# A two-layer hybrid encoder on one core: the matrix-inverse bursts ordered behind the query-key products, a free slot between two of them, an early square-root table, and wider last multiplications

## The chip, the core and the metric

The kernel runs on one core of a Trainium2 chip, in float32. The metric is device microseconds of one execution. The kernel before took 2420.61 us, the median of three runs (2418.82, 2420.61 and 2422.45).

## The reference

Two layers work on 1040 rows (16 meta tokens and 1024 tokens) of width 1024. Each layer normalises its rows, projects them once, and splits the projection between a gated delta rule of 4 heads in both directions and a gated short convolution; both go through one output projection into the residual. A SwiGLU block of 22 tiles of 128 follows. Of the delta rule, this matters here:

```
q, k, v, g, beta = (to_chunks(t) ...)            # chunks of 64 in the reference
decay_mat = exp(where(incl, G_i - G_j, -inf))
M = where(strict, (k*beta) k^T * decay_mat, 0);  A = M + I
u = A^-1 (v*beta);  w = A^-1 (k*beta*exp(G))     # the triangular inverse
attn = (q k^T) * decay_mat                       # the query-key products
step: v_new = u - w S;  o = (q*exp(G)) S + attn v_new;  S = S*gl + k_dec^T v_new
o = (o_fwd + o_bwd);  o = o * rsqrt(mean(o*o) + eps)
...
h = rmsnorm(h, final_norm_w);  return h[:, N_META:]
```

## The kernel before, in words

Everything is stored transposed, with channels on the 128 partitions and rows along the free dimension. A dense product keeps float32 accuracy by splitting each operand in a rounded part and a remainder: `dense` issues three matmuls per k tile (lines 174, 175 and 176) into a PSUM bank `pacc` (or `pf`), over column chunks of 348, 346 and 346 (layer 0) or 512, 512 and narrower ones (layer 1). Weights arrive by SyncE's queue (line 137), are split by ScalarE (line 138) and VectorE (line 139), and go into a ring of three.

The small work of the delta rule is done under these dense products. The chunks here are of 128 rows, nine in all, the first with the 16 meta rows. Three lists of jobs, `jobs`, `jobs2` and `jobs3`, are emptied by `slot()` inside `dense`, one entry of each list per slot; `None` is a free slot. A projection of three chunks has three slots, after each 24 matmuls. So the lists set where small work stands between dense work, and a priority (`mmp`, moved on by `low`) keeps it there when the scheduler orders each engine's instructions. The order on an engine is in the end that of the scheduler, by priorities and by its own estimate of when operands are ready; it then is fixed in the program.

`jobs2` holds, from the first z projection on, the query-key products: `chunk_a(c)` issues four 128x128 products per chunk (line 597), loads the two directions' decay matrices on GpSimd's queue (line 600), multiplies on VectorE (line 601) and stores the result to DRAM (line 602).

`jobs3` holds the inverse of the 128x128 triangular matrices, by blocks of 32, of both directions and all chunks at once (`invert`). Its matmuls are short and come in bursts: the first form (`first(0)` and `first(1)`, line 677) has 64 products of 32x32 in each half; the second and third form (lines 692 and 693) have four parts of 48; the fourth and the fifth (lines 718 and 738) have 64 of 64x64 each. float32 operands that are not rounded go through TensorE in two passes, so that 64 such products are 128 matmuls and 128 weight loads in the trace. Each burst is given to `low(f, hold=True)`, which orders its first matmul behind the last dense matmul issued so far (`after(one, last_mm[0])`); nothing orders it against query-key products.

Then comes the scan over the chunks (`scan_step`, all its matmuls on line 968, the meta chunk's on 1047), the two directions interleaved, nine steps. From step 4 on the second direction to reach a chunk finishes it (`finalize`): the first one's output is stored to DRAM (`od`, line 1028) and loaded back (line 1102), VectorE takes off the state's part (line 1103) and adds the PSUM bank (line 1104), ScalarE squares and sums (line 1108), then takes the square root (line 1110), for which it first loads another activation table; VectorE takes the reciprocal and scales (lines 1111 and 1112), TensorE transposes (line 1114). The bank that line 1104 reads is the one that the next step's second state product of that direction writes. ScalarE copies with a scale on lines 996, 1004 and 1005 serve each step. `St` is the state, `qs` the state's part of the output, `vv` the new values, `b3f`/`a3f` the row that is finished.

At the very end of layer 1 the rows are multiplied by the final norm's factor, in three column parts. For the last part (256 columns) eight multiplications of 128x256 follow a reciprocal (line 1900), six on VectorE and two on GpSimd (line 1863), and eight stores go out in turn on SyncE's and ScalarE's queues (line 1864). Line 1974 stands for what closes the program: each engine drains and all meet.

Of the kernel before, what the change touches and what calls it, by code (L numbers as in the profile page):

```python
# [7 lines left out]
F32 = mybir.dt.float32  # L8
# [7 lines left out]
KT = 8  # L16
NMETA = 16
L = 1040
H = 4
# [23 lines left out]
def trunk(ctx: ExitStack, tc: tile.TileContext, xT, w_in, w_ba, w_out, w_gu, w_dn,  # L43
# [41 lines left out]
    def after(ins, prev):  # L85

        if prev is not None:
            tc.add_manual_dep(ins.ins, prev.ins.name, dep, reason="order")
        return ins

    def at_prio(p):
        tc.cur_priority = p
# [239 lines left out]
    for l in range(DEPTH):  # L332
# [258 lines left out]
        def chunk_a(c):  # L591

            if c == 0:
                return None if last else chunk_a0()
            n, s0 = span(c)
            qk = bank("b").rearrange("p (h i) -> p h i", h=4)
            low(lambda: [mm(qk[0:n, h, 0:n], KTt[:, h, s0:s0 + n], QT[:, h, s0:s0 + n], start=True, stop=True) for h in range(H)])
            for d in (0, 1):
                dt_ = t2k("dt")
                qdma(dt_[0:n, :, 0:n], dtd[c, d].rearrange("p (h i) -> p h i", h=4)[0:n, :, 0:n])  # L600
                tt(out=dt_, in0=qk[0:n, :, 0:n], in1=dt_[0:n, :, 0:n], op=ALU.mult)
                dma(aqd[c, d], dt_.rearrange("p a b -> p (a b)"))
# [2 lines left out]
        B = [slice(32 * b, 32 * b + 32) for b in range(4)]  # L605

        inv = {}

        def sub_start():

# [24 lines left out]
        def invert():  # L635
# [5 lines left out]
            def turn_back(d):  # L641
                rows, cols = (Xi[:, d], Xi[:, d].rearrange("p i c -> p c i"))[::1 - 2 * d]
                after(nc.vector.transpose(out=XB[d].rearrange("p q c -> p c q"), in_=cols), evacs[-1])
                nc.vector.transpose(out=ZB[:, d].rearrange("p q i -> p i q"), in_=rows)
                for b in range(4):
                    act(out=Pv[d][B[b], :, B[b]], in_=ZB[B[b], d], func=AF.Copy)
# [6 lines left out]
            def fill():  # L653
                for d, f, s in (pairs[0], pairs[2]):
                    fo, so = 32 * (f % 2), 32 * (s % 2)
                    nc.vector.tensor_copy(XF[B[f], :, fo:fo + 32], XB[d][B[f]])
                    nc.vector.tensor_copy(XF[B[s], :, so:so + 32], XB[d][B[s]])
                    nc.vector.memset(XF[B[f], :, so:so + 32], 0.0)
# [10 lines left out]
            def first(part):  # L669
                if part == 0:  # L670
                    banks_["1"] = [view(bank("f"), 32) for _ in halves]
                pss = banks_["1"]

                def turn(q):
                    out = []
                    for i in range(2):
                        out += [mm(pss[i][B[s ^ 2 * i], q, :], Pv[d][B[f], 16 * i + q, B[s]], XB[d][B[f], 16 * i + q, :], **kw) for (d, f, s) in pairs]
                    return out

                low(lambda: [turn(q) for q in range(8 * part, 8 * part + 8)][0][0], True)  # L680
                if part == 1:
                    act(out=QS[:, halves[0], :], in_=pss[0], func=AF.Copy, scale=-1.0)
                    act(out=QS[H64[0], halves[1], :], in_=pss[1][H64[1]], func=AF.Copy, scale=-1.0)
                    act(out=QS[H64[1], halves[1], :], in_=pss[1][H64[0]], func=AF.Copy, scale=-1.0)
# [44 lines left out]
            def fifth():  # L729
# [12 lines left out]
                for j in range(4):  # L742
# [5 lines left out]
                        else:  # L748
                            nc.vector.tensor_copy(to, ps)

            return ([lambda: turn_back(0), lambda: (turn_back(1), fill()), None] + [lambda i=i: first(i) for i in range(2)] + [None] + [lambda qs=qs, i=i: second_third(qs, i) for qs in halves for i in range(2)]
                    + [None, fourth, None, fifth])

        l2s = {}
# [102 lines left out]
        def low(f, hold=False):  # L857

            here = tc.cur_priority
            at_prio(mmp[0])  # L860
            one = f()
            if hold:
                after(one, last_mm[0])
            mmp[0] = tc.cur_priority
            at_prio(here)

        def v_store(i, v, c0):

# [71 lines left out]
        bk = [[bank("f"), bank("f")], [bank("b"), bank("b")]]  # L940
        fin = row(Y[1] + "f")
        nfin = [0]
        done = set()
        read = {}

# [5 lines left out]
        def scan_step(d, c, first, final, tied=False, behind=None):  # L951
            n, s0 = 128, 16 + 128 * (c - 1)
            base = (1 - d) * 2048
            V, K, A, sz = (rec[:, base + 512 * i:base + 512 * i + 512].rearrange("p (h e) -> p h e", h=4) for i in range(4))
            dma(V[0:n].rearrange("p h e -> p (h e)"), vkd[c, 0:n, 0, :])
            if not final:
                dma(K[0:n].rearrange("p h e -> p (h e)"), vkd[c, 0:n, 1, :])
            dma(A.rearrange("p h e -> p (h e)"), aqd[c, d])
            Zs = [Pv[d][:, (c - 1) * 4 + h, :] for h in range(4)]
            As = [A[:, h, :] for h in range(4)]  # L960
            b0, b1 = (v4(t) for t in bk[d])
            opened = [None]

            def group(ph):
                opened[0] = ph

            def gm(*args, **kw):
                one = mm(*args, **kw)  # L968
                if opened[0] is not None and tied:
                    after(one, ready[1 - d].get(opened[0]) if tied == 1 else ends[1 - d])  # L970
                if opened[0] == "A":
                    after(one, behind)
                opened[0] = None
                ends[d] = one
                return one

            vv = vvs[d]
            vn, vs = v4(vv[:, 0:512]), v4(vv[:, 512:1024])
            if first:
                r = V  # L980
            else:
                ks = b0
                group("A")
                for h in range(H):
                    gm(ks[0:n, h, :], KTt[:, h, s0:s0 + n], St[d][:, h, :], start=True, stop=True)
                r = vn
                for h in range(H):
                    ready[d]["B"] = stt(out=r[0:n, h, :], in0=ks[0:n, h, :], scalar=negE[0:n, d, c, h:h + 1], in1=V[0:n, h, :], op0=ALU.mult, op1=ALU.add)
            qs = None
            if not first:  # L990

                qs = qso[d]
                for h in range(H):
                    gm(b1[0:n, h, :], QT[:, h, s0:s0 + n], St[d][:, h, :], start=True, stop=True)
                for h in range(H):
                    act(out=qs[0:n, h, :], in_=b1[0:n, h, :], func=AF.Copy, scale=negE[0:n, d, c, h:h + 1])
            yield
            vr = b1
            group("B")
            for h in range(H):  # L1000
                gm(vr[0:n, h, :], Zs[h], r[0:n, h, :], start=True, stop=True)
            for h in range(H):
                if not final:
                    ready[d]["C"] = act(out=vs[0:n, h, :], in_=vr[0:n, h, :], func=AF.Copy, scale=bkd[0:n, d, c, h:h + 1])
            ready[d]["C"] = read[d, c] = act(out=vn[0:n], in_=vr[0:n], func=AF.Copy)
            yield
            group("C")
            if not final:
                su = b0
                for h in range(H):  # L1010
                    gm(su[:, h, :], K[0:n, h, :], vs[0:n, h, :], start=True, stop=True)
            po = b1
            for h in range(H):
                gm(po[0:n, h, :], As[h], vn[0:n, h, :], start=True, stop=True, skip_group_check=True)
            if not final:
                for h in range(H):
                    if first:
                        ready[d]["A"] = nc.vector.tensor_copy(St[d][:, h, :], su[:, h, :])
                    else:
                        ready[d]["A"] = stt(out=St[d][:, h, :], in0=St[d][:, h, :], scalar=gl[:, d, c, h:h + 1], in1=su[:, h, :], op0=ALU.mult, op1=ALU.add)  # L1020
            pof = po.rearrange("p h e -> p (h e)")
            if c not in done:
                done.add(c)
                if first:
                    act(out=vs.rearrange("p h e -> p (h e)"), in_=pof, func=AF.Copy)
                else:
                    tt(out=vs, in0=po, in1=qs, op=ALU.subtract)
                dma(od[c], vs.rearrange("p h e -> p (h e)"))
            else:
                finalize(c, n, s0, pof, qs, sz)  # L1030
# [820 lines left out]
        else:  # L1851
# [46 lines left out]
                    pend = [lambda q=q, n0=n0, n1=n1, mul=tt if n0 == 16 and q > 5 else ptt: scaled(q, n0, n1, mul, ss[:, n0:n1], dma) for q in range(KT)]  # L1898
            act(out=sv, in_=ps[:, 0:n1 - n0], func=AF.Sqrt, scale=1.0 / D, bias=cols["eps"])
            nc.vector.reciprocal(out=sv, in_=sv)  # L1900
            for q in range(KT):
                scaled(q, n0, n1, ptt if q in (3, 6) else tt, sv, (dma, adma)[q % 2])
        if not last:
            finish_bc(ss, 0, L, rsd[1])
        hsrc = hd
# [73 lines left out]
```

## Time and profile before

| | |
|---|---|
| runs | 2418.82, 2420.61, 2422.45 us |
| profiled execution | 2422.96 us, span 2421.1 us |
| TensorE busy (matmul, weight load) | 2401.0 us (99%), 2225.8 us (92%) |
| VectorE, ScalarE, GpSimd busy | 1836.5, 1043.6, 89.7 us |
| mean granted TensorE clock | 0.997 |
| moved by DMA | 336.57 MB, 139 GB/s |
| first bursts of the inverse, line 677 | 228.5 to 1453.6 us, 512 matmuls in both layers |

A row of the timeline gives start, length, engine, line, operation, the tiles written and read, the shape and how many instructions are merged; in square brackets stands how long the engine was idle before it and what ended that. Matmuls overlap, so the distance of two starts is what a matmul costs, not its length. Times are counted from the span's start; layer 0's inverse runs at 228 to 262 us, its scan to about 490 us, and layer 1's inverse begins at 1440 us.

### The profile page before, as it was taken

To read this page: it belongs to the slowest core of one execution; us is meant where nothing else is said; L and a number is where in the kernel's file an instruction comes from. 1 tells how busy PE (TensorE), PEld (TensorE's weight loads), DVE (VectorE), ACT (ScalarE), POOL (GpSimd) and SP (SyncE) were. 2 spreads that over 40 slices of the span, in tenths; PEclk is the share of its full clock that TensorE was granted. 3 is DMA by queue.
4 is the path that set the end of the run, shared out by engine and by line. 5 is a ranking of instruction groups with operands and counts; after the bars stand their busy time and mean duration, and the time that the engine had idled before them with its cause. 6 is when DMAs were issued, how large, how long until landed. Compare 5 with 4: busy or idle time off the path is not lost.

```text
span 2421.1 us, 44848 instructions
## 1 busy us (share of the span) xinstructions
PE 2401.0 (99%) x17507; PEld 2225.8 (92%) x17507; DVE 1836.5 (76%) x3322; ACT 1043.6 (43%) x1959; POOL 89.7 (4%) x195
## 2 busy tenths in 40 slices
PE   9999999999999999999999999999999999999998
PEld 8999999999999999999999988998988888888887
DVE  7798545768888877877658985457898887778775
ACT  6654334436233333444446432335553343334544
POOL 0141000000000000000001200000000000000002
PEclk9999999999999999999999999999999999999999
DMA  4455444633222224674224445446433232347641
GB/s 136 147 164 177 164 137 139 200 112 130 93 100 86 101 74 136 223 254 142 88 87 152 156 151 174 140 136 213 138 114 111 81 111 79 121 154 246 198 126 70
DMA packets 198023, 336.57 MB, mean 139 GB/s; under 512 B 22972, under 2 KB 88692, under 8 KB 197812
## 3 DMA queue, kind: packets, MB, share of 16 engines
q1 hardware_dynamic: 174324, 294.06, 36.6%
q10 hardware_dynamic: 18464, 25.85, 3.1%
q0 software_dynamic: 5024, 13.82, 1.9%
q8 instruction: 137, 2.24, 0.4%
q14 instruction: 74, 0.61, 0.1%
HBM read 251.52 MB, written 82.12 MB: 138 GB/s over the span
## 4 chain that ended last, share of the span: by engine, by line
PE 93%; DVE 3%; DMA 2%; issue 1%; ACT 1%; SPq 0%; DVEq 0%; ACTq 0%
PE pacc L174 10%; PE pacc L176 10%; PE pacc L175 10%; PE pacc L1269 4%; PE pacc L1273 4%; PE pacc L1272 4%; PE pb L1273 3%; PE pb L1269 3%; PE pb L1272 3%; PE pf L1269 3%; PE pf L1273 3%; PE pf L1272 3%; PE pf L968 3%; PE pb L968 3%; PE pacc L1837 2%; PE pacc L1836 2%
## 5 line engine op out<-in xcount | busy, mean ns | idle before, releaser
L174 PE MATMUL pacc<-a,whi 128*128 128x346 f32 (+1 forms) x800 | 261.1, 327 | 0.6 <-ACT a L210 0.4
L176 PE MATMUL pacc<-a,wlo 128*128 128x346 f32 (+1 forms) x800 | 259.5, 325 | 0.1
L174 PE MATMUL pacc<-b,whi 128*128 128x342 f32 (+3 forms) x672 | 232.3, 346 | 0.0
L176 PE MATMUL pacc<-b,wlo 128*128 128x342 f32 (+3 forms) x672 | 230.6, 344 | 0.0
L175 PE MATMUL pacc<-a,whi 128*128 128x346 f32 (+1 forms) x681 | 221.8, 326 | 0.5 <-DVE a L211 0.5
L138 ACT ACTIVATE whi<-raw 128x512 fp32r<-128x512 f32 x166 | 104.7, 631 | 249.1 <-PE pacc L175 179.7
L175 PE MATMUL pacc<-b,whi 128*128 128x342 f32 (+3 forms) x580 | 199.7, 344 | 0.0
L139 DVE TENSOR_TENSOR wlo<-raw,whi 128x512 fp32r<-128x512 f32 x166 | 114.1, 687 | 63.1 <-ACT whi L138 61.6
L174 PEld LDWEIGHTS pacc<-a,whi 128*128 128x128 f32 x800 | 151.0, 189 | 3.6 <-issue 1.5
L176 PEld LDWEIGHTS pacc<-a,wlo 128*128 128x128 f32 x800 | 151.0, 189 | 1.3 <-issue 0.6
L174 PEld LDWEIGHTS pacc<-b,whi 128*128 128x128 f32 x672 | 126.4, 188 | 10.3 <-issue 1.7
L176 PEld LDWEIGHTS pacc<-b,wlo 128*128 128x128 f32 x672 | 126.5, 188 | 9.8 <-issue 1.5
L175 PEld LDWEIGHTS pacc<-a,whi 128*128 128x128 f32 x681 | 128.7, 189 | 4.7 <-issue 1.9
L175 PEld LDWEIGHTS pacc<-b,whi 128*128 128x128 f32 x580 | 109.2, 188 | 7.2 <-issue 1.1
L1251 ACT ACTIVATE whi<-rw 128x512 fp32r<-128x512 f32 (+1 forms) x84 | 51.7, 620 | 105.4 <-PE pacc L1272 28.2
L1251 ACT ACTIVATE b<-rw 128x512 fp32r<-128x512 f32 (+1 forms) x63 | 38.8, 620 | 89.9 <-PE pb L1272 35.3
L1251 ACT ACTIVATE a<-rw 128x512 fp32r<-128x512 f32 (+1 forms) x63 | 38.5, 619 | 71.0 <-PE pacc L1272 29.3
L351 DVE TENSOR_TENSOR a<-pacc,rstd 128x342 f32<-128x342 f32 (+3 forms) x59 | 32.4, 553 | 38.3 <-PE pacc L176 36.9
L1252 DVE TENSOR_TENSOR wlo<-rw,whi 128x512 fp32r<-128x512 f32 (+1 forms) x84 | 56.2, 672 | 6.6 <-ACT whi L1251 6.2
L1837 PE MATMUL pacc<-P,wlo 128*128 128x260 f32 (+1 forms) x177 | 59.4, 336 | 0.0
L1836 PE MATMUL pacc<-P,whi 128*128 128x260 f32 (+1 forms) x177 | 59.3, 335 | 0.0
L1834 PE MATMUL pacc<-P,whi 128*128 128x260 f32 (+1 forms) x177 | 59.2, 335 | 0.0
(1178 smaller groups left out, 7858.2 us busy)
## 6 DMA issues: line engine op xcount, KB each, us to landing
raw<-in_w_in SPq DMA_DIRECT2D x110, 256.0 KB
raw<-in_w_gu SPq DMA_DIRECT2D x106, 256.0 KB
rw<-in_w_gu SPq DMA_DIRECT2D x90, 256.0 KB
rw<-in_w_dn SPq DMA_DIRECT2D x90, 192.0 KB
raw<-in_w_out SPq DMA_DIRECT2D x48, 256.0 KB
b<-ad SPq DMA_DIRECT2D x45, 260.0 KB
a<-ad SPq DMA_DIRECT2D x45, 256.0 KB
ad<-a SPq DMA_DIRECT2D x20, 520.0 KB
```

The lines of the kernel that those rows point to most:

```text
L138: whi_done[0] = hasten(wpr, lambda: act(out=hi, in_=raw[:, 0:kk, :], func=AF.Copy))
L139: whi_done[1] = hasten(wpr, lambda: tt(out=lo, in0=raw[:, 0:kk, :], in1=hi.bitcast(F32), op=ALU.subtract))
L174: mm(ps[:, :n], wh, xh[:, n0:n1], start=(seen[0] == 1), stop=False)
L175: mm(ps[:, :n], wh, xl[:, n0:n1], start=False, stop=False)
L176: last_mm[0] = mm(ps[:, :n], wl, xh[:, n0:n1], start=False, stop=(seen[0] == K))
L968: one = mm(*args, **kw)
L1251: hasten(wpr, lambda: act(out=hi, in_=src, func=AF.Copy))
L1269: one = mm(ps[:, :CW], w[0][:, k, :], th[:, cs], start=first and k == 0, stop=False, skip_group_check=True)
L1272: mm(ps[:, :CW], w[0][:, k, :], tl[:, cs], start=False, stop=False, skip_group_check=True)
L1273: one = mm(ps[:, :CW], w[1][:, k, :], th[:, cs], start=False, stop=stop and k == nk - 1, skip_group_check=True)
L1836: mm(ps[:, :CW], wh[:, k, :], tl[:, cs], start=False, stop=False, skip_group_check=True)
L1837: mm(ps[:, :CW], wl[:, k, :], th[:, cs], start=False, stop=en, skip_group_check=True)
```

## The change

Four edits. `chunk_a` keeps the last of its four products in `qk_last`, and `low(f, hold=True)` orders the burst's first matmul behind that product too. In `invert`'s list a free slot stands between `first(0)` and `first(1)`, so all that follows in `jobs3` comes one slot later. In the scan, at step 4 of direction 0, ScalarE takes the square root of a constant into a new tile `root`, ordered behind that step's last copy of line 996. At the end, the last column part is multiplied by five VectorE instructions, three of two rows of tiles at once (128x2x256) and two of one, with five stores; GpSimd has no part in it.

```
-            low(lambda: [mm(qk[0:n, h, 0:n], ...) for h in range(H)])
+            qk_last[0] = low(lambda: [mm(qk[0:n, h, 0:n], ...) for h in range(H)])[-1]
...
-  ... + [lambda i=i: first(i) for i in range(2)] + [None] + ...
+  ... + [lambda: first(0), None, lambda: first(1), None] + ...
...
             if hold:
                 after(one, last_mm[0])
+                after(one, qk_last[0])
...
+            halfway = c == 4 and d == 0
...
                 for h in range(H):
-                    act(out=qs[0:n, h, :], in_=b1[0:n, h, :], func=AF.Copy, scale=negE[0:n, d, c, h:h + 1])
+                    copied = act(out=qs[0:n, h, :], in_=b1[0:n, h, :], func=AF.Copy, scale=negE[0:n, d, c, h:h + 1])
+                if halfway:
+                    after(act(out=root, in_=epsc, func=AF.Sqrt), copied)
...
-            for q in range(KT):
-                scaled(q, n0, n1, ptt if q in (3, 6) else tt, sv, (dma, adma)[q % 2])
+            for i, (q, w) in enumerate(((0, 2), (2, 2), (4, 2), (6, 1), (7, 1))):
+                h = hb[q // 4][:, q % 4:q % 4 + w, n0:n1]
+                tt(out=h, in0=h, in1=sv.unsqueeze(1).to_broadcast([128, w, n1 - n0]), op=ALU.mult)
+                (dma, adma)[i % 2](out[q:q + w, :, n0 - 16:n1 - 16].rearrange("q p e -> p q e"), h)
```

What it moves is seen in the order of the engines' instructions. TensorE, layer 0, in the first half of the inverse's first form; `pf` are the burst's banks, `pb` those of the query-key products of two chunks. Before:

```order
L677 MATMUL pf_2492<-e_2170,P_853 32x32 x2
L677 MATMUL pf_2492<-e_2171,P_854 32x32 x2
L677 MATMUL pf_2493<-e_2170,P_853 32x32
L597 MATMUL pb_2389<-b_36_211,b_37_212 128x128 x4
L677 MATMUL pf_2493<-e_2170,P_853 32x32
L677 MATMUL pf_2493<-e_2171,P_854 32x32 x2
L677 MATMUL pf_2492<-e_2170,P_853 32x32 x2
L677 MATMUL pf_2492<-e_2171,P_854 32x32 x2
L677 MATMUL pf_2493<-e_2170,P_853 32x32 x2
L677 MATMUL pf_2493<-e_2171,P_854 32x32
L597 MATMUL pb_2479<-b_36_211,b_37_212 128x128 x4
```

And now, where the burst's line is 678 by the added lines:

```order
L176 MATMUL pacc_2558<-a_3_74,wlo_2422 128x346
L597 MATMUL pb_2389<-b_36_211,b_37_212 128x128 x4
L597 MATMUL pb_2479<-b_36_211,b_37_212 128x128 x4
L678 MATMUL pf_2492<-e_2170,P_853 32x32 x2
L678 MATMUL pf_2492<-e_2171,P_854 32x32 x2
L678 MATMUL pf_2493<-e_2170,P_853 32x32 x2
```

Both groups of query-key products now stand ahead of the burst, behind ten more dense matmuls, and its 64 products follow one another. Between the two halves stood 10 dense matmuls; now 24 do, and one more group of four. In layer 1 two groups and two groups of transposes (line 882) stood within the first half and one group within the second; none does now, and 31 dense matmuls and one group stand between the halves.

VectorE, layer 0, around the first chunk that is finished (step 4 of the scan); `b3f` is the row that is finished, `pf_4175` the bank that its next state product writes, `vv_4173` serves the other direction. Before:

```order
L364 SCALAR_TENSOR_TENSOR b_403_3794<-b_384_3612,par,b_403_3794 128x1039
L1103 TENSOR_TENSOR b3f_4178<-b3f_4178,qs_4170 128x512
L365 SCALAR_TENSOR_TENSOR b_403_3794<-b_384_3612,par,b_403_3794 128x1039
L988 SCALAR_TENSOR_TENSOR vv_4173<-pb_4176,negE_585,b_180_1491 128x128 x4
L1103 TENSOR_TENSOR b3f_4178<-b3f_4178,qs_4171 128x512
L1104 TENSOR_TENSOR b3f_4178<-pf_4175,b3f_4178 128x512
```

And now, seven lines further down in the file:

```order
L365 SCALAR_TENSOR_TENSOR b_403_3794<-b_384_3612,par,b_403_3794 128x1039
L1110 TENSOR_TENSOR b3f_4178<-b3f_4178,qs_4170 128x512
L1111 TENSOR_TENSOR b3f_4178<-pf_4175,b3f_4178 128x512
L993 SCALAR_TENSOR_TENSOR vv_4173<-pb_4176,negE_585,b_180_1491 128x128 x4
L1110 TENSOR_TENSOR b3f_4178<-b3f_4178,qs_4171 128x512
L993 SCALAR_TENSOR_TENSOR vv_4172<-pf_4174,negE_585,b_180_1491 128x128 x4
```

The addition that frees the bank follows its subtraction at once. On TensorE the product that writes this bank stood 41 dense matmuls behind the three products ahead of it, and now stands 17 behind them; those three stand 27 dense matmuls behind the step before, where there were 22.

ScalarE at the same place, before and now, with the square root's table:

```order
L996 ACTIVATE qs_4171<-pb_4177,negE_585 128x128 x4
L1108 ACTIVATE pa_4557,st_4558<-b3f_4178 128x128 x4
L1110 ACT_TABLE_LOAD
L1110 ACTIVATE st_4558<-st_4558 128x4
L996 ACTIVATE qs_4170<-pf_4175,negE_585 128x128 x4
```

```order
L1001 ACTIVATE qs_4170<-pf_4175,negE_585 128x128 x4
L1003 ACT_TABLE_LOAD
L1003 ACTIVATE root_4179<-epsc 128x1
L1011 ACTIVATE vv_4173<-pb_4177,bkd_587 128x128 x4
```

The table is loaded one step earlier, behind the copies of line 996 (now 1001) and ahead of those of line 1004 (now 1011); there are as many table loads as before.

More of the change, by code (lines that the diff above doesn't have):

```diff
@@ L596, in chunk_a @@
             qk = bank("b").rearrange("p (h i) -> p h i", h=4)
-            low(lambda: [mm(qk[0:n, h, 0:n], KTt[:, h, s0:s0 + n], QT[:, h, s0:s0 + n], start=True, stop=True) for h in range(H)])
+            qk_last[0] = low(lambda: [mm(qk[0:n, h, 0:n], KTt[:, h, s0:s0 + n], QT[:, h, s0:s0 + n], start=True, stop=True) for h in range(H)])[-1]
             for d in (0, 1):
@@ L607, in trunk @@
         inv = {}
+        qk_last = [None]
         def sub_start():
@@ L749, in fifth @@
                             nc.vector.tensor_copy(to, ps)
-            return ([lambda: turn_back(0), lambda: (turn_back(1), fill()), None] + [lambda i=i: first(i) for i in range(2)] + [None] + [lambda qs=qs, i=i: second_third(qs, i) for qs in halves for i in range(2)]
+            return ([lambda: turn_back(0), lambda: (turn_back(1), fill()), None] + [lambda: first(0), None, lambda: first(1), None] + [lambda qs=qs, i=i: second_third(qs, i) for qs in halves for i in range(2)]
                     + [None, fourth, None, fifth])
@@ L863, in low @@
                 after(one, last_mm[0])
+                after(one, qk_last[0])
             mmp[0] = tc.cur_priority
             at_prio(here)
+            return one
         def v_store(i, v, c0):
@@ L942, in trunk @@
         nfin = [0]
+        root = sb.tile([128, 1], F32, tag="root", name=nm("root"))
         done = set()
```

## The prediction

> **What bounds the kernel now.** I read the page first: busy time, code queue and chain.
>
> ```profile
> span 2421.1 us, 44848 instructions
> PE 2401.0 (99%) x17507; PEld 2225.8 (92%) x17507; DVE 1836.5 (76%) x3322; ACT 1043.6 (43%) x1959; POOL 89.7 (4%) x195
> q8 instruction: 137, 2.24, 0.4%
> PE 93%; DVE 3%; DMA 2%; issue 1%; ACT 1%; SPq 0%; DVEq 0%; ACTq 0%
> ```
>
> TensorE is busy for 99% and 93% of the chain is its own. The change leaves every matmul in, so only three things can move the time: moments in which TensorE stands still, stretches in which it runs slowly, and the end, where it is done. The view of waits, TensorE's alone, names the moments:
>
> ```profile
> PE pf L677 <- issue: 1.6, 1, 1.6
> PE pa L1114 <- ACT qs L996: 1.4, 1, 1.4
> PE pf L968 <- DVE b3f L1104: 0.6, 1, 0.6
> ```
>
> The longest lies in the inverse's burst, with no engine behind it ("issue"); the next two lie at one step of the scan. All three places are touched.
>
> **The bursts of layer 0.** TensorE's timeline there:
>
> ```profile
> 228.45 0.33 PE L677 MATMUL pf<-e,P 32*32 32x32 f32 x26
> 228.72 1.16 PE L597 MATMUL pb<-b,b 128*128 128x128 f32 x8
> 229.81 0.31 PE L677 MATMUL pf<-e,P 32*32 32x32 f32 x20
> 230.18 1.13 PE L597 MATMUL pb<-b,b 128*128 128x128 f32 x8
> 231.23 0.90 PE L677 MATMUL pf<-e,P 32*32 32x32 f32 x82
> 232.07 0.43 PE L176 MATMUL pacc<-a,wlo 128*128 128x346 f32 x1
> 233.86 0.92 PE L677 MATMUL pf<-e,P 32*32 32x32 f32 x85
> 236.38 0.57 PE L677 MATMUL pf<-e,P 32*32 32x32 f32 x43 [1.60 <-issue]
> 236.89 0.42 PE L174 MATMUL pacc<-a,whi 128*128 128x348 f32 x1
> 242.34 1.05 PE L597 MATMUL pb<-b,b 128*128 128x128 f32 x8
> ```
>
> The same stretch in the view of windows (length, TensorE, weight load, VectorE, ScalarE, GpSimd, granted clock, DMA share, GB/s), and what the code queue moved from 233.8 to 234.8 us:
>
> ```profile
> 234.80:236.40 1.60, 0.02 (x4) 0.02 (x4) 0.00 (x0) 0.00 (x0) 0.60 (x2) 1.00 1.00 297
> 236.40:237.80 1.40, 1.40 (x49) 1.36 (x50) 0.60 (x1) 0.00 (x0) 0.00 (x0) 1.00 0.89 309
> 237.80:241.30 3.50, 3.50 (x14) 3.50 (x14) 3.50 (x6) 2.83 (x4) 0.54 (x1) 0.51 0.81 284
> ```
>
> ```profile
> q8 instruction: 1, 0.02, 5.5%
> ```
>
> I read the pause as a wait for code. TensorE's 17507 matmuls and as many weight loads are 35014 instructions, and queue 8 moved 137 packets, so one packet is 256 instructions. Half a first form (26 + 20 + 82 matmuls with their loads) is one whole packet, used up in little over a microsecond. One packet was moving just before the pause ended, with the DMA engines at a share of 1.00. Counting 128 matmuls back from the pause: 85 of the second half, 10 dense, 33 of the first half's last 82, so the packet that ran out was begun at about 231.7 us, the next arrived at 236.4, and the way from asking to having took at most about 4.6 us here. A packet must last that long.
>
> Then from 237.8 us for 3.5 us the granted clock is 0.51: 14 matmuls where there is room for 22. About half of the 3.5 us is lost, 1.7 us.
>
> [...]
>
> **The change there.** Ten more dense matmuls and two groups of four products (16 matmuls, two passes each) now come ahead of the first burst, so that the packet's start, formerly 33 matmuls from the end of the first half, lies 59 from it. Up to the next packet's start come: 59 matmuls of the first half (0.6 us at 0.84 us for 82, from 231.23 to 232.07), 24 dense (3.8 us: 0.16 each, from the 10 between 232.07 and 233.86 with their change-over), one group (0.9 us: 0.8 to the next dense start and 0.1 for a slower successor), and 37 of the second half (0.4): 5.7 us against at most 4.6. The pause goes: **-1.6 us**, and with it the half-clock stretch: **-1.7 us**. The margin is 1.1 us; DMA work hides nothing here, it is what could lengthen the way of the code. The free slot's own cost is nil on TensorE: the dense products that fill it are the same ones, earlier; what is late next by it, the fourth and fifth form, starts the scan within a few dense matmuls of where it stood.
>
> Interrupted bursts also cost. The second half without its pause takes 236.89 - 233.86 - 1.60 = 1.43 us; a group between dense ones 0.9. So the first half should take 1.43 + 1.8 = 3.23, and took 3.62 (228.45 to 232.07): 0.4 lost. Layer 1:
>
> ```profile
> 1440.66 0.24 PE L677 MATMUL pf<-e,P 32*32 32x32 f32 x2
> 1440.84 0.66 PE L882 MATMUL pa<-ident,a3f 128*128 128x128 f32 x4
> 1445.54 0.50 PE L174 MATMUL pacc<-b,whi 128*128 128x512 f32 x1
> 1451.26 0.26 PE L677 MATMUL pf<-e,P 32*32 32x32 f32 x6
> 1453.71 0.50 PE L174 MATMUL pacc<-b,whi 128*128 128x512 f32 x1
> ```
>
> The first half takes 4.88 us with two groups of products and two of transposes inside (about 0.5 each): 4.23 expected, 0.65 lost. The second takes 2.45 against 2.33: 0.1. Together **-1.2 us**, between 0 (if the change-overs are paid wherever the groups stand) and 1.5.
>
> **The scan's step 4.** VectorE, TensorE and ScalarE in layer 0:
>
> ```profile
> 385.01 1.06 PE L968 MATMUL pf<-S,b 128*128 128x128 f32 x8
> 388.94 0.69 DVE L1103 TENSOR_TENSOR b3f<-b3f,qs 128x512 f32<-128x512 f32 x1 [4.21 <-DMA b3f<-od]
> 392.39 0.68 DVE L1104 TENSOR_TENSOR b3f<-pf,b3f 128x512 f32<-128x512 f32 x1
> 393.13 1.16 PE L968 MATMUL pf<-S,b 128*128 128x128 f32 x8 [0.56 <-DVE b3f L1104]
> 394.83 1.28 ACT L1110 ACT_TABLE_LOAD   x1
> 396.57 0.69 DVE L1112 TENSOR_TENSOR b3f<-b3f,st 128x512 f32<-128x512 f32 x1
> 397.41 0.63 PE L1114 MATMUL pa<-ident,b3f 128*128 128x128 f32 x4 [1.39 <-ACT qs L996]
> ```
>
> TensorE stands 0.56 us for line 1104, then 1.39 us for a transposition that waits through the table load (the releaser named, line 996, came after the root on ScalarE; the data came from line 1112). In the new order the table load lies between copies that wait for TensorE anyway, and its 1.28 us are off this path: the transposition stands 17 dense matmuls and one group of products behind the bank product and should wait 0.2 at most. But the product on the bank now comes 17 dense matmuls after 385.9 us plus 0.8 us for the five that moved ahead: TensorE is there at about 389.4. The row lands at 388.94, perhaps 0.3 later since line 364 now stands ahead of the state update, and lines 1103 and 1104 now run back to back (1.3 us): the bank is free at 390.5. So TensorE waits 1.1 us here. Net: 1.95 before, 1.3 after, **-0.6 us**; the ends are -1.9 (all hidden) and +2 (row later by 2.6 us). Layer 1 shows no wait at this step, and its bank product moves five dense matmuls back: nothing.
>
> **The end.** From the timeline, and from the views of lines 1863 and 1974 (count: shortest/median/longest ns, first and last start):
>
> ```profile
> 2404.94 4.72 POOL L1863 TENSOR_TENSOR b<-b,rstd 128x256 f32<-128x256 f32 x6
> ...
> 2410.47 1.75 DVE L1900 RECIPROCAL rstd<-rstd 128x256 f32<-128x256 f32 x1 [1.75 <-ACT rstd L1899]
> 2412.26 3.16 DVE L1863 TENSOR_TENSOR b<-b,rstd 128x256 f32<-128x256 f32 x6
> 2412.31 1.83 POOL L1863 TENSOR_TENSOR b<-b,rstd 128x256 f32<-128x256 f32 x2 [2.65 <-DVE rstd L1900]
> ```
>
> ```profile
> L1863 DVE TENSOR_TENSOR b<-b,rstd x6: 412/420/947, 2412.3 to 2415.0; 128x256 f32<-128x256 f32 x6
> ```
>
> ```profile
> L1974 POOLq DRAIN  x3: 51/98/7991, 2412.3 to 2420.8; - x3
> L1974 SPq DRAIN  x3: 7/7/7, 2418.3 to 2420.5; - x3
> ```
>
> SyncE, which waits for the stores, is done at 2418.4. GpSimd's drain runs 7.99 us, from 2412.3 to 2420.3, six after its last multiplication (2414.14), and only then do the engines meet. The new end has no work on GpSimd behind 2409.7 (the earlier column part), so its drain should end by 2417.7 at the latest. VectorE needs at most three of 128x512 (0.69 by line 1103) and two of 128x256 (0.42, the median; the 0.95 lie beside GpSimd's): 2.9 us for 3.16. The last store goes out 0.3 us or a little more earlier and SyncE is done at about 2418.0. So the end moves by 2420.3 - 2418.0: **-2.3 us**. The ends are 0, if the drain is not due to those two instructions, and 2.4.
>
> **Sum.** 1.6 + 1.7 + 1.2 + 0.6 + 2.3 = 7.4 us against the profiled execution's own time of 2422.96 (span 2421.1 and 1.9 around it): 2415.6. That execution is 2.35 us above the median of the runs, 2420.61, whose own spread is 3.6. I take it that some runs lack the half-clock stretch or part of the pause, and count 1.5 us less for the median: 2420.61 - 5.9 = 2414.7. About 0.2% (4.8 us) is what a measurement of this kernel can tell from no change; the line is at 2415.8, close by.
>
> **The rivals.**
> - *The drain stays.* GpSimd's long drain is not due to the two multiplications. For: nothing in the trace shows the same drain without them. Against: VectorE's and TensorE's drains end with their own last work. The gain is then 3.6: 2417.0, within 0.2%.
> - *The pause moves.* Another packet's start falls badly, in a burst that had luck before (layer 1's fifth form is followed by the scan's small products at once), or the code's way is longer than 5.7 us. 3.3 us less gain: 2418.0.
> - *The pause is not for code.* Then it comes again with the second half, as above, 2418.0. Against: 256 instructions per packet, and the packet in flight.
> - *The bank product waits long* (slower). It stands 17 dense matmuls back instead of 41, so 3.8 us of cover are gone; the stored row goes out at 380 us and is back at 389, and every microsecond past 388.1 now stops TensorE. To be over 0.2% slower it must cost 10.7 us, the row some 8 us later plus another half-clock stretch: 2425.5. Against: the trace has the row in 9 us under the same loads.
>
> [...]
>
> **Chances.** Forecast 0.55; drain stays 0.17; pause moves 0.12; not for code 0.06; bank product waits long 0.05; mixtures 0.05. Faster by over 0.2%: most of the forecast's case (0.52) and a part of the others (0.08), 0.6. Slower by over 0.2%: 0.05. Same: 0.35. Range 2411.5 to 2419.5: below, the whole 7.4 off the median, the scan's better end (1.3 more) and the bursts' (0.3); above, each of the three rivals that gain less, and most of two of them together (2420.3).
>
> **What would show it.** Right: no "issue" wait on line 678, a granted clock of 1.00 through the inverse, 128 matmuls of the first form in one row, no table load ahead of the first root, a wait of about 1 us for line 1111, GpSimd's drain over before SyncE's. Wrong: a drain still ending at the span's end less 0.8 us, a pause in another burst, or waits of several microseconds on line 972.

## The result, and the profile after

| | before | after |
|---|---|---|
| median of twelve runs beside each other | 2421.47 us | 2415.22 us |
| range | 2418.60 to 2423.49 | 2413.41 to 2417.59 |
| ratio, 95% interval | | 0.9975 [0.9968, 0.9983] |
| profiled execution, span | 2422.96, 2421.1 us | 2415.47, 2413.7 us |
| granted TensorE clock | 0.997 | 0.998 |

The changed kernel is faster by 0.25%, about 6.1 us (4.1 to 7.7); 5.9 were forecast. The two profiled spans differ by 7.4 us, the forecast sum. That the sum is met is partly luck: two of its terms were missed by more than a microsecond, in opposite directions.

The page of the changed kernel, the same lines as of before:

```profile
span 2413.7 us, 44833 instructions
PE 2398.2 (99%) x17507; PEld 2224.1 (92%) x17507; DVE 1835.0 (76%) x3321; ACT 1044.8 (43%) x1961; POOL 87.9 (4%) x193
q8 instruction: 137, 2.24, 0.4%
PE 95%; DVE 2%; DMA 1%; ACT 1%; issue 0%; SPq 0%; DVEq 0%; ACTq 0%; POOLq 0%
```

TensorE's waits now:

```profile
PE pb L597 <- DVE dt L601: 1.5, 1, 1.5
PE pa L267 <- DVE sel L318: 1.1, 1, 1.1
...
PE pa L1121 <- ACT qs L1001: 0.3, 1, 0.3
```

The wait for "issue", the one for the addition and the one behind the square root's table have left the head of the list (the transposition, now line 1121, keeps 0.3 us, in layer 1). A new wait leads it, on line 597, a query-key product; line 267, which follows, is a warm-up product at the start.

**The bursts of layer 0.** TensorE's timeline without the dense matmuls, and VectorE at the wait:

```profile
229.38 1.95 PE L597 MATMUL pb<-b,b 128*128 128x128 f32 x16
231.26 1.29 PE L678 MATMUL pf<-e,P 32*32 32x32 f32 x128
238.11 1.13 PE L597 MATMUL pb<-b,b 128*128 128x128 f32 x8 [1.54 <-DVE dt L601]
239.17 1.29 PE L678 MATMUL pf<-e,P 32*32 32x32 f32 x128
```

```profile
237.27 0.69 DVE L601 TENSOR_TENSOR dt<-pb,dt 128x512 f32<-128x512 f32 x1 [2.69 <-DMA dt<-dtd]
```

Both halves run in one row of 128, without a pause. But the third group of query-key products, which stood at 242.34 us before, now stands ahead of the second half, and it can't write its bank until VectorE's line 601 has read an earlier group out of it; that multiplication had waited 2.69 us for a decay matrix to arrive. The view of windows (length, TensorE, weight load, VectorE, ScalarE, GpSimd, granted clock, DMA share, GB/s) over two stretches of 3.41 us, the first with the wait in it:

```profile
234.64:238.05 3.41, 1.93 (x13) 1.63 (x11) 0.78 (x2) 0.00 (x0) 0.35 (x1) 1.00 0.90 322
238.05:241.46 3.41, 3.35 (x143) 3.22 (x144) 2.92 (x4) 1.00 (x2) 0.54 (x1) 1.00 0.85 300
```

Unlike before, no stretch at half clock follows.

**The scan's step 4, layer 0**: SyncE's store and reload of the first chunk's row, then VectorE and TensorE.

```profile
380.82 0.38 SPq L1035 DMA_DIRECT2D od<-vv  x1
384.97 0.32 SPq L1109 DMA_DIRECT2D b3f<-od  x1
...
385.85 1.06 PE L972 MATMUL pf<-S,b 128*128 128x128 f32 x8
...
387.45 0.69 DVE L1110 TENSOR_TENSOR b3f<-b3f,qs 128x512 f32<-128x512 f32 x1 [4.69 <-DMA b3f<-od]
388.25 0.69 DVE L1111 TENSOR_TENSOR b3f<-pf,b3f 128x512 f32<-128x512 f32 x1
...
389.45 1.05 PE L972 MATMUL pf<-S,b 128*128 128x128 f32 x8
```

The addition is over at 388.94, the product on its bank starts at 389.45, and waits for nothing. The same two SyncE rows before:

```profile
380.33 0.39 SPq L1028 DMA_DIRECT2D od<-vv  x1
...
386.37 0.32 SPq L1102 DMA_DIRECT2D b3f<-od  x1
```

From store to reload it was 6.0 us before and is 4.15 now.

**The end.** GpSimd's and VectorE's last work, and the drains (count: shortest/median/longest ns, first and last start):

```profile
2403.01 1.59 POOL L1870 TENSOR_TENSOR b<-b,rstd 128x256 f32<-128x256 f32 x2
...
2405.41 1.75 DVE L1907 RECIPROCAL rstd<-rstd 128x256 f32<-128x256 f32 x1 [1.75 <-ACT rstd L1906]
2407.20 2.57 DVE L1910 TENSOR_TENSOR b<-b,rstd 128x512 f32<-128x512 f32 x5
```

```profile
L1983 POOLq DRAIN  x3: 51/98/12286, 2398.4 to 2413.2; - x3
L1983 SPq DRAIN  x3: 7/7/7, 2412.6 to 2413.0; - x3
```

GpSimd's drain now runs 12.29 us, longer than the 7.99 before, but from 2398.4: it is over at 2410.7, before SyncE is done at 2412.6. From the last reciprocal to the span's end it was 2421.1 - 2410.47 = 10.6 us and is 8.3.

**Where the 7.4 us lie**, by the start of the same dense matmul in both traces: 0.6 are there before the inverse begins (at 222 us), where nothing has changed. Layer 0's inverse brings 2.0 (2.6 in all at 280 us), its scan 1.9 (4.5 at 500); 0.6 more come in the long matmul stages up to layer 1's inverse (5.1 at 1440), where nothing has changed either. Layer 1's inverse and scan bring 0.6; the long stages after them give 0.6 back; the end brings 2.3.

### The profile page after: what moved, and what is told of

Same layout as the page of the kernel before. It is cut to its first block, busy times and chain, and to the rows that moved or that the text cites. A ratio compares the mean times of both kernels' runs of the same rounds, so it can differ in the third digit from the quotient of the medians.

```text
span 2413.7 us, 44833 instructions
## 1 busy us (share of the span) xinstructions
PE 2398.2 (99%) x17507; PEld 2224.1 (92%) x17507; DVE 1835.0 (76%) x3321; ACT 1044.8 (43%) x1961; POOL 87.9 (4%) x193
## 4 chain that ended last, share of the span: by engine, by line
PE 95%; DVE 2%; DMA 1%; ACT 1%; issue 0%; SPq 0%; DVEq 0%; ACTq 0%; POOLq 0%
PE pacc L174 11%; PE pacc L175 11%; PE pacc L176 10%; PE pacc L1276 4%; PE pacc L1280 4%; PE pacc L1279 4%; PE pb L1280 3%; PE pb L1276 3%; PE pb L1279 3%; PE pf L972 3%; PE pf L1276 3%; PE pf L1280 3%; PE pf L1279 3%; PE pb L972 3%; PE pacc L1843 2%; PE pacc L1841 2%
```

## The experiments

Ratios are to runs of the kernel before on the same chip, with 95% intervals; one per mille is 2.4 us. The two kernels of experiments 3 and 4 were run once each, for their traces: 2428.94 us with 19 products, 2423.38 with one.

| kernel | ratio | profiled span |
|---|---|---|
| the end alone | 0.9988 [0.9979, 0.9997] | 2416.9 |
| early root alone | 1.0002 [0.9993, 1.0011] | 2426.5 |
| order and slot | 0.9991 [0.9983, 1.0000] | 2417.2 |
| order without slot | 1.0013 [1.0004, 1.0022] | 2423.4 |
| slot without order | 0.9991 [0.9983, 1.0000] | 2420.7 |
| changed kernel without root | 0.9979 [0.9969, 0.9988] | 2413.9 |
| changed kernel again | 0.9977 [0.9967, 0.9986] | 2415.5 |
| changed, one GpSimd operation more | 0.9992 [0.9983, 1.0001] | 2420.5 |
| changed, a slot behind the third chunk | 0.9963 [0.9949, 0.9977] | 2411.4 |
| the same again | 0.9965 [0.9953, 0.9978] | 2412.6 |

**1. The end alone.**

```
+            for i, (q, w) in enumerate(((0, 2), (2, 2), (4, 2), (6, 1), (7, 1))):
...
+                tt(out=h, in0=h, in1=sv.unsqueeze(1).to_broadcast([128, w, n1 - n0]), op=ALU.mult)
```

> The kernel before with the change's end alone. Theory (the closing drain is set by GpSimd's last operation, which ended at 2414.1 us and here ends with the column part before): 2.3 us less (2.0 to 2.6) from the last part's reciprocal to the span's end, 10.6 -> 8.3 us, GpSimd's drain over before SyncE's; the pause of 1.6 us and the wait for the square root's table stay as they are. Rival (the drain is due to something else, the end is set by the stores): 0 to -0.3 us.

From the reciprocal (2408.85) to the span's end (2416.9) it is 8.05 us, 2.5 less than before, and the drains' rows read as in the changed kernel:

```profile
L1976 POOLq DRAIN  x3: 51/98/12292, 2401.9 to 2416.6; - x3
L1976 SPq DRAIN  x3: 7/7/7, 2416.1 to 2416.4; - x3
```

The time agrees (2.9 us less, 0.7 to 5.1). So the end is worth its forecast by itself.

**2. One small GpSimd operation more at the end.** To the changed kernel:

```
+            ptt(out=pick[:, 0, 0:1], in0=h[:, 0, 0:1], in1=h[:, 0, 0:1], op=ALU.mult)
```

> The changed kernel with one more operation at the end: a 128x1 product on GpSimd that reads the last multiplied row of VectorE (its result is read by nothing). Theory (GpSimd's closing drain ends 6.1 us after its last operation, whatever that was): the drain ends about 2416.0 us, the span about 0.8 us later: +3.1 us against the changed kernel (2.5 to 3.7). Rival (the long drain of before came of the two large multiplications and their amount of work): +0 to +0.3 us.

```profile
2408.60 1.75 DVE L1907 RECIPROCAL rstd<-rstd 128x256 f32<-128x256 f32 x1 [1.75 <-ACT rstd L1906]
...
2413.13 0.19 POOL L1912 TENSOR_TENSOR pick<-b 128x1 f32<-128x1 f32 x1 [5.34 <-DVE b L1910]
```

```profile
L1984 POOLq DRAIN  x3: 51/98/6349, 2413.1 to 2420.0; - x3
L1984 SPq DRAIN  x3: 7/7/7, 2415.8 to 2419.7; - x3
```

The operation takes 0.19 us and ends at 2413.32; the drain ends at 2413.10 + 6.35 = 2419.45, 6.1 later, while SyncE was done at 2415.8. The end is 2420.5 - 2408.6 = 11.9 us long, 3.6 over the changed kernel's 8.3. In the changed kernel the drain ends 2410.7 - 2404.60 = 6.1 us after GpSimd's last multiplication, before the change 2420.3 - 2414.14 = 6.1. So the 6.1 us are the same behind last work of 0.19, 1.59 and 1.83 us. (The span shows more than 3.6, in part because a half-clock stretch fell into this execution, see the end of 8.)

**3 and 4. The pause, shifted.** Only the number of warm-up products at the start is changed. Between them and the burst TensorE has the same instructions as before, from 66 us on in the same order too. Behind the burst that does not hold throughout: in the kernel with 19 the scheduler ordered the scan otherwise. The pause lies ahead of that.

```
-    for _ in range(11):
+    for _ in range(19):
```

> The kernel before with 19 warm-up products instead of 11 on line 266 (16 more matmuls and 16 more weight loads at the very start, everything behind in the same order). Theory (TensorE's code comes in packets of 256 instructions, 128 matmuls with their loads, and the pause stands where one begins): the pause moves 16 matmuls forward in the program, the second half of the first form in layer 0 splits 69 and 59 instead of 85 and 43. Rival (the pause comes from the data or the transfers at that time): it stays behind the 85th, or goes where the time puts it.

The other run has `range(1)`.

> The same with one warm-up product instead of 11 (20 matmuls fewer). Theory: the pause moves 20 matmuls back, the second half splits 105 and 23. Rival: as in the run with 19.

With 19:

```profile
232.15 0.90 PE L677 MATMUL pf<-e,P 32*32 32x32 f32 x82
234.75 0.79 PE L677 MATMUL pf<-e,P 32*32 32x32 f32 x69
237.02 0.71 PE L677 MATMUL pf<-e,P 32*32 32x32 f32 x59 [1.48 <-issue]
```

With one:

```profile
231.40 0.90 PE L677 MATMUL pf<-e,P 32*32 32x32 f32 x82
234.02 1.09 PE L677 MATMUL pf<-e,P 32*32 32x32 f32 x105
236.33 0.32 PE L677 MATMUL pf<-e,P 32*32 32x32 f32 x23 [1.22 <-issue]
```

69 and 59, 105 and 23: to the matmul. Counted from the program's start, TensorE goes on with its 1750th matmul in both, in the kernel before, and in every other profile with a pause in this burst. A pause for the burst's data would not move with instructions that ran 230 us earlier. The pause keeps its place in the count of TensorE's instructions. Their code comes at about 256 to a packet: in the kernel before, from 500 to 1400 us, queue 8 moved 56 packets while 7104 matmuls and 7103 weight loads ran, 254 to each. That a packet begins at this count is the prediction's reading. Counting 128 matmuls back, as there, the packet took 4.6 us in the first run and 4.3 in the second; in the kernel with the end alone, whose bursts are those of before,

```profile
231.53 0.90 PE L677 MATMUL pf<-e,P 32*32 32x32 f32 x82
...
235.32 0.57 PE L677 MATMUL pf<-e,P 32*32 32x32 f32 x43 [0.26 <-issue]
```

it took 3.4, and the pause is 0.26. With early root alone it is 4.8, and 1.7. So the pause is not a constant: 0.26, 1.22, 1.48, 1.60 and 1.73 us in the five profiles with the bursts of before, as the code comes sooner or later. In each of them queue 8 moved one packet meanwhile: it began to move 1.0 us (the end alone) to 2.5 us (early root alone) behind the packet's start, was over 0.9 to 1.0 us later, and TensorE went on 1.3 to 1.6 us after that. So most of what the five pauses differ by lies in the time until the packet moves.

**5. The order without the slot.** To the kernel before:

```
+            qk_last[0] = low(lambda: [mm(qk[0:n, h, 0:n], ...) for h in range(H)])[-1]
...
+                after(one, qk_last[0])
```

> The order alone, without the free slot. In layer 0 both halves of the first form then stand back to back, 256 short matmuls without a dense one between. Theory (a packet of 256 instructions must last about 4.6 us): two packets are used up in 2.6 us, so TensorE stands with the releaser issue within these 256 matmuls, 2 to 5 us in all, more than the 1.6 of before; +1 to +3 us against before, less what the whole bursts bring. [...]

```profile
231.85 2.11 PE L678 MATMUL pf<-e,P 32*32 32x32 f32 x213
236.97 0.57 PE L678 MATMUL pf<-e,P 32*32 32x32 f32 x43 [3.01 <-issue]
```

```profile
PE pf L678 <- issue: 4.4, 2, 3.0
```

The pause stands behind 213 = 128 + 85 matmuls, the same place in the program as before, but with no dense matmuls between the halves it is 3.0 us, with a clock of 0.50 from 238.07 to 241.49 us behind it; a second pause, of 1.4 us, comes in layer 1, where only seven dense matmuls and a group stand between the halves. Slower than before by 3.1 us (1.0 to 5.3), as the theory had it: with the interruptions alone cured the pause is 3.0 us and not 1.60.

**6. The slot without the order, and both.**

> The free slot alone, without the order behind the query-key products. In layer 0 the first half still has two groups inside (26, 20 and 82 matmuls), but 34 dense matmuls and a group stand between it and the second. Theory (a packet must last about 4.6 us, and the dense matmuls between the halves make it last): no pause, no half-clock stretch; no group between the halves that waits more than the 0.2 us of a group with its bank free; the 1.28 us for the table go in layer 0 with the slot and come in layer 1: -2.5 to -4 us in the profile. Rival (the order behind the products is what took the pause away): the pause of 0.3 to 1.7 us stays, 0 to -1 us.

> The bursts' half of the change alone (order behind the query-key products, and the free slot). Theory: pause and half-clock stretch go (-3.3), bursts run whole (-0.5 to -1.2), the third group of products stands 1.5 us for its bank (+1.5), the bank product of the scan's step 4 doesn't wait (-0.56) but the transposition behind the table load does (1.4 as before, or less where more dense matmuls lie ahead of it): -3 to -4 us in the profile, no issue wait in the burst. Rival (what the trace after gained there was not the bursts' doing): -1 us or less.

Neither has an issue wait in the bursts, neither a half-clock stretch, and both gain the same, 2.2 us (0 to 4.1). So it is the free slot that takes the pause away. In the profiles order and slot bring 3.9 us and the slot alone 0.4, less than expected of it, but of these 3.5 us 1.2 are there before the inverse, where the two kernels do the same. What the order adds to the slot is below what the times can tell; the traces show it in place. By the same dense matmuls, the kernel with both gains 0.8 us over the slot alone in layer 0's inverse and 1.0 in layer 1's, where the slot alone leaves the first halves interrupted; this is one pair of profiles. Both have the new wait of line 597, 1.4 and 1.5 us, which was not expected of the slot alone: it comes with the slot.

**7. The early square root.** Alone:

> The kernel before with the early square root alone; VectorE keeps the order in which another operation stands between the subtraction of the state's part and the addition of the bank. Theory (the table load alone held the transposition): the wait of 1.39 us goes, the 0.56 us for the bank stay: -1.4 us, too little to be told from no change by the time, to be seen in the waits. Rival (both waits come of VectorE's order): both stay, 0 us.

```profile
PE pf L969 <- DVE b3f L1108: 0.9, 1, 0.9
PE pa L1118 <- ACT qs L998: 0.3, 1, 0.3
```

The transposition's wait goes from 1.4 to 0.3 and the bank's grows from 0.6 to 0.9: 0.8 us by the trace, not the expected 1.4, and too little for the time. The bank's wait is no constant: with the same order in the scan it is 1.0 us in the profile of the end alone and nothing in that of one warm-up product, where the transposition's is 1.4 and 1.3. (Its profiled span holds 3.7 us more than before at 472 us, a late reload and behind it a clock of 0.50 from 474.20 to 477.61 us; the runs do not bear that out.) And the changed kernel without it:

> The changed kernel without the early square root. Theory (the table's load is seen only in layer 1, where the order and the slot have moved the transposition close behind it): a wait of 1.3 us for line 1114's transposition in layer 1 instead of 0.2, none in layer 0: +1.1 us against the changed kernel. Rival (the early root was needed in layer 0 too): two such waits, +2.4 us.

```profile
PE pb L597 <- DVE dt L601: 1.3, 1, 1.3
PE pa L1117 <- ACT qs L999: 1.3, 1, 1.3
```

One wait of 1.3 us, and it is layer 1's:

```profile
1615.92 1.28 ACT L1113 ACT_TABLE_LOAD   x1
...
1618.51 0.63 PE L1117 MATMUL pa<-ident,a3f 128*128 128x128 f32 x4 [1.27 <-ACT qs L999]
```

In layer 0 none is left. The new order and slot alone cure layer 0's two waits and make one in layer 1 (1.4 us in experiment 6's kernel with both, 1.1 with the slot alone), which the early root then takes away (0.3 us of it remain in the profile above, nothing in the second one of the changed kernel). The times, 0.9979 and 0.9977, can't show it.

**8. The new wait, and its cure.** The changed kernel again, and with one more empty slot in the list of the query-key products:

```
-                jobs2.extend(sum([[lambda c=c: chunk_a(c), None] for c in ca], []))
+                jobs2.extend(sum([[lambda c=c: chunk_a(c), None] + [None] * (i == 2) for i, c in enumerate(ca)], []))
```

> The changed kernel with one more empty slot in the list of the query-key products, behind the third chunk. In layer 0 a group that stood between the halves then stands right behind the first half, and the group behind it comes after the second half; in layer 1 31 dense matmuls instead of 7 stand ahead of the group between the halves. Theory (the 1.5 us for the bank of line 597 are the price of the group's early place): the wait goes, -1.5 us against the changed kernel, about 2413.7. Rival (the group right behind the first half finds its bank no freer): the wait stays or grows, 0 to +1.5 us.

> The changed kernel once more, beside the others on the same chip: 0.9975 of before, the wait of line 597 in layer 0 between 1.3 and 2 us; where it is over about 1.5 us within one window of 3.41 us, a half-clock stretch of 3.41 us follows it.

> The changed kernel with the empty slot behind the third chunk once more, now on the same chip as the changed kernel. Theory: no wait in the inverse, 1.5 to 3 us less than the changed kernel (3 where this would have had a half-clock stretch behind its wait). Rival (its earlier lead was the chip's): within 1 us of it.

The changed kernel, run again, waits 1.7 us on line 597. With the slot behind the third chunk (the second of the two runs, on the same chip as the changed kernel):

```profile
229.87 1.05 PE L597 MATMUL pb<-b,b 128*128 128x128 f32 x8
230.85 1.29 PE L678 MATMUL pf<-e,P 32*32 32x32 f32 x128
232.07 1.15 PE L597 MATMUL pb<-b,b 128*128 128x128 f32 x8
236.97 1.29 PE L678 MATMUL pf<-e,P 32*32 32x32 f32 x128
```

No wait is left in the inverse. The median is 2414.22 us (2413.72 to 2414.46) against 2417.29 (2415.20 to 2418.62): 3.1 us less, with no overlap. By the same dense matmuls, 2.0 us are gained in layer 0's inverse, 1.9 in the first pair of profiles; the rest is spread and not explained. This version is faster than both kernels: by its ratios 9.0 and 8.5 us under before.

**The idle time ahead of the half-clock stretches.** The execution with 19 warm-up products and the changed kernel run again, the windows with the pause or the wait, each with the one behind it:

```profile
234.42:237.83 3.41, 1.93 (x132) 1.56 (x131) 0.00 (x0) 0.63 (x1) 2.14 (x4) 1.00 0.93 306
237.83:241.24 3.41, 3.41 (x13) 3.41 (x14) 2.22 (x4) 1.07 (x1) 0.54 (x1) 0.50 0.83 287
```

```profile
233.93:237.34 3.41, 3.13 (x20) 2.83 (x18) 1.47 (x2) 0.17 (x1) 1.48 (x3) 1.00 0.83 217
237.34:240.75 3.41, 2.02 (x121) 1.93 (x124) 2.86 (x4) 0.00 (x0) 0.54 (x1) 1.00 0.87 344
```

Ahead of the end the traces hold seven half-clock stretches. In the kernel before, the stretch is 3.413 us long; the clock is first full at 5.73 us and halves at 237.84, 68 times that length later. In the executions with two stretches they begin 69 times that length apart: at 237.83 and 473.35 us with 19 products, at 238.68 and 474.20 with early root alone. Cut into steps of 3.41 us that meet them, the seven come behind steps with 1.48 (the run with 19 products, 3.41 less 1.93 busy), 1.60, 1.73, 2.13, 2.22, 2.25 and 2.31 us idle. None came behind the same 1.48 us in the changed kernel's first profile, also inside one step (234.64 to 238.05 above), nor behind 1.67 us that fell across a boundary (237.06 to 238.73 in the changed kernel run again, 0.28 and 1.39 us of it in the two steps). So at 1.48 us idle in 3.41 it went either way, and the changed kernel stands there: in the execution of experiment 2 the wait of line 597 was 2.1 us and the clock fell to 0.50 at 241.26.

## Why the prediction was right, and where not

*The pause* (-1.6) and *the half-clock stretch* (-1.7): right in place and cause, since in experiments 3, 4 and 5 the pause keeps its place in the count of instructions, and right in size for this pair of profiles. That the stretch would go with the pause was the author's estimate from one trace; of the five pauses in the profiles with the bursts of before, those of 1.48, 1.60 and 1.73 us have a stretch behind them, those of 0.26 and 1.22 us none. The price of the stretch can be read alone: the kernel with the end alone runs the same program through this burst without the stretch, and gains 3.0 us there, 1.34 of them by its shorter pause. "At most about 4.6 us" (4.7 by the starts of the matmuls) was one draw out of 3.4 to 4.8. Two readings on the way were wrong. The packet of queue 8 did not move "just before the pause ended" but from 233.90 to 234.78, up to its begin; TensorE went on 1.6 us later. And the packet's start came to lie 43 matmuls from the end of the first half, not 59, since the two groups had stood ahead of its last 82 matmuls already. 53 matmuls of the second half instead of 37 make up for that, so the 5.7 us stand; with the new wait it became 7.6. The forecast's allowance, "some runs lack the half-clock stretch or part of the pause", is borne out: three of the five profiles with the bursts of before have the stretch, the five pauses are 1.26 us on average, and the medians differ by 6.25 us where the spans differ by 7.4, 1.2 less; 1.5 were allowed.

*The cost of the groups that moved.* This step failed. "A group between dense ones 0.9" priced the third group by groups whose banks were free. Ahead of the second half it came 1.5 us too soon for its bank, and with the slot's own cost put at "nil" nothing in the sum stood for that: a loss of 1.5 us. The rows were there: two groups' worth of line 601, each needing a matrix over busy DMA (a share of 0.90 in the stretch with the wait), had to be over first. Experiment 8 shows the price by taking it away.

*Interrupted bursts* (-1.2): 0.5 and 0.2 us in layer 0's two halves (3.62 to 3.09, 1.43 to 1.22), and 0.9 in layer 1 if all that it gained besides the 0.3 of its new wait is counted here: 1.6. Experiment 6 has 0.8 and 1.0 us for the order in one pair of profiles, about the same; in the times it was not shown, where the slot without the order measured the same.

*The scan* (-0.6): the mechanism, a shorter cover for the bank product, was right, and TensorE is there 3.6 us after the product ahead of it where 3.5 were forecast. The row, taken to land as late as before, comes 1.6 us after that product and not 3.3, since its reload goes out 4.15 us after its store and not 6.0. In the eight profiles with the slot this is 3.8 to 4.5 us, with the order alone 4.3, in the five with the bursts of before 4.8 to 6.3; why was not tried. So no wait of 1.1 is left, and both waits of layer 0 go: -1.95 (0.3 come back in layer 1). The 0.56 of the bank was itself a draw out of 0 to 1.0, by the profiles in experiment 7. "Layer 1 ... nothing" was wrong too: it has a wait of 1.3 without the root, 0.3 or none with it. The root's table load was credited to layer 0; it pays in layer 1.

*The end* (-2.3): measured 2.3, and 2.5 alone. The rival by which the drain stays is refuted by experiments 1 and 2, as that of a pause not for code is by 3 and 4. The pause did not move to another burst in the changed kernel, and the bank product did not wait.

So of 7.4 us the pause and its stretch brought 3.3, the end 2.3, the scan 1.7, the bursts up to 1.6; the new wait took 1.5. These terms are good to about half a microsecond: in layer 0's inverse they add up to 2.5, and the same dense matmuls show 2.0. What came and went where nothing had changed (0.6 before the inverse, 0.6 and -0.6 in the long stages) is as large. The misses in the scan and the groups cancel, which is luck.

## What to carry to other kernels

In these traces 128 short matmuls with their loads, a packet's worth of code, took 1.3 us, and in the five profiles with the bursts of before TensorE went on with the next packet 3.4 to 4.8 us after it began one: the long burst needed long matmuls around it, and with its interruptions alone cured it stood for 3.0 us. An instruction that is moved earlier brings its bank and its operands' arrivals with it (1.5 us on line 597), so ask who last reads that bank and what that reader waits for. GpSimd's drain ended 6.1 us after GpSimd's last work, so in this program that work had to be over at least that long before the last store was done.

## What the runs showed of the hardware that was not expected

- GpSimd's closing drain ended 6.1 us after GpSimd's last operation, where that was a 128x256 multiplication (before, and in the changed kernel) and where it was 0.19 us of a 128x1 one (experiment 2). In experiment 2 SyncE, with all stores, was done 3.6 us ahead of it.
- The code of a packet of 256 instructions took between 3.4 and 4.8 us from the begin of the packet ahead of it in the five profiles with the bursts of before, and the same instructions paused for 0.26 to 1.73 us. TensorE went on 1.3 to 1.6 us after the packet had landed; the rest of the spread lies before the packet moves. The mean DMA share over the 3.41 us with the pause was 0.93 at 1.48 us, 0.93 at 1.60 and 0.90 at 1.73, so it does not tell them apart.
- Behind steps of 3.41 us with 1.60 to 2.31 us of TensorE idle the clock was 0.50 for the 3.41 us that followed, which cost 1.7 us in the kernel before; behind 1.67 us idle across two steps it stayed at 1.00, and 1.48 us within a step went either way (0.50 with 19 products, 1.00 in the changed kernel).
